# Twelve buffers for x tiles, weight casts ahead of tile 1, four tiles transposed on TensorE in a hybrid encoder block

## The chip, the cores and the metric

The kernel runs on one core of one Trainium2 chip. The metric is the device time of one execution, in microseconds (us). Most executions of a kernel agree within 0.3%.

## What is computed

One layer of a bidirectional encoder. The rows of x (2048 x 1024) are normalised and multiplied by one wide matrix; its columns give a Fourier branch, a branch of dilated window attention (24 heads in three configurations), and gates; an output projection and the residual follow.

```python
hn = rms_norm(h, norm_w)
proj = hn @ w_in.astype(jnp.float32)
u_f, g_f, q, k, v, g_a = jnp.split(proj, SPLIT_POINTS, axis=-1)
...
q = rms_norm(q.reshape(B, S, N_ATTN_HEADS, HEAD_DIM), q_norm_w) * HEAD_DIM ** -0.5
k = rms_norm(k.reshape(B, S, N_ATTN_HEADS, HEAD_DIM), k_norm_w)
...
for c, (window, dilation) in enumerate(DILATED_CONFIGS):
    o_c, lse_c = dilated_window_attention(q[:, :, sl], k[:, :, sl], v[:, :, sl], window, dilation, slopes)
...
y_a = o * jax.nn.silu(g_a)
mixed = jnp.concatenate([y_f, y_a], axis=-1) @ w_out.astype(jnp.float32)
h = h + mixed
```

## The kernel before

The 2048 rows of x are 16 tiles of 128 rows. Each float32 operand of a large product is split into two float16 halves, a high one and a low one, and the product is the sum of three: high by high, low by high, high by low. For that the normalised x must lie transposed in `xT`, both halves (j = 0 and 1) of all 16 tiles.

**A tile of x** goes through these steps. `x_load` (L174) brings it into the float32 buffer `xs` by a DMA from SP; `xs` has six places and tile r takes place r % 6. `x_sq` (L187) squares it on ScalarE and sums each row. `x_rs` makes the reciprocal root of the sums on VectorE, in 11 small steps (L195, L105 to L112), for a group of tiles that `xgrp` names: tile 0 alone, 1 and 2, 3 alone, then pairs. `x_hi` (L210) writes the high half on ScalarE, `x_lo` (L218) the low half on VectorE. A half is transposed either on TensorE, eight blocks of 128 x 128 (`x_tr`, L225) and an eviction to `xT` (`x_ev`, L230) on ScalarE or VectorE, or by a transposing DMA from SP (`x_dt`, L233). Tiles 0 and 1 take TensorE for both halves; from tile 2 on the high half takes TensorE and the low half the DMA.

**A unit** is two heads of one configuration: 384 columns of w_in. Its weights are eight tiles of 128 rows (k = 0 to 7): `w_load` (L243) brings them from SP, `w_prep` reduces them to one scale (L259 to L278: a reduce for each tile, a small matmul into `pm`, the scale `nws`) and writes the high halves on ScalarE (L284) and the low halves on VectorE (L286). `w_prep` is a generator of 20 steps. `inproj(u, t)` (L307) then makes 24 matmuls of 128 x 384 for tile t, of about 0.16 us each at full clock, into one of three `psq` buffers. For tile 0 of unit 0 they come in the order high by high (8), low by high (8), high by low (8); otherwise k by k.

**The order is written out by hand.** A start-up block works tile 0, the weights of unit 0 and tile 1 by single steps (`go(...)` takes one step of a generator). After it one loop runs over all products, iteration i holding `inproj` number i; unit 0 is iterations 0 to 15. Each iteration takes the steps of many stages in a fixed order: the value half and the sums of tile i - 1 (L318 to L346), the low half's DMA, the high and low halves of tile i + 3, two or three transposes between the matmuls, queries and keys of tile i - 6 (L359 to L371 on GpSimd and ScalarE, transposed by DMA at L380 and copied across partitions at L401), and from iteration 14 the attention of unit 0 (`att_s` at L444 and L456 on TensorE, `att_max` at L474, `att_exp` at L492, `att_hi`, `att_lo`, and the DMA at L509). The function `plan` says how many steps of the next unit's `w_prep` each iteration takes: for unit 1 it begins at iteration 2, with 14 iterations left. Each engine and each issuing queue takes its instructions in this order.

`gains` (L154 to L170) makes the key gains on VectorE, writes them to DRAM (`KD`) and reads them back to all partitions (`kb`) by DMAs from SP.

**Areas.** `xs` lies in the first of two areas with the tag `st`; the units' transposed queries and keys (`st`) take the two in turn.

```python
self.xs = self.stp.tile([128, 3, 2, S], F16, name="xs", tag="st", bufs=2)
```

The attention of a unit, the other branch and the output follow in the loop and in `tail_`; the change does not touch them.

Of the kernel before, what the change touches and what calls it, by code (L numbers as in the profile page):

```python
# [24 lines left out]
NT = 16  # L25
# [51 lines left out]
def plan(n):  # L77
    if n == 14:
        return [3, 3, 2, 1, 0, 1, 0, 1, 2, 2, 2, 1, 1, 1]
    if n < 12:  # L80
        return [4, 4, 1, 1, 1, 3, 3, 3]
    head = [2, 2, 2, 2, 1, 1, 1] if n == 16 else [3, 3, 2, 1, 1, 1]
    m = n - len(head)
    return head + [9 // m + (i < 9 % m) for i in range(m)]
# [6 lines left out]
class Kernel:  # L91
# [81 lines left out]
    def x_load(self, r):  # L173
        self.nc.sync.dma_start(self.xs[:, r % 6], self.a["x"][0, r * 128:r * 128 + 128])  # L174

    def xgrp(self, r):
        return ((0, 1), (1, 2), (1, 2), (3, 1))[r] if r < 4 else (r - r % 2, 2)

    def x_sq(self, r):
        r0, n = self.xgrp(r)  # L180
        if r == r0:
            self.XS[r0] = self.sm.tile([128, 2], F32, name="xss", bufs=6)
            self.XR[r0] = self.sm.tile([128, 2], F32, name="xri", bufs=6)
        junk = self.wk.tile([128, 2, 256], F32, name="xjk", tag="P", bufs=2)
        junk = junk.rearrange("p a d -> p (a d)").bitcast(F16)
        o = r - r0
        self.nc.scalar.activation(junk, self.xs[:, r % 6], AF.Square, accum_out=self.XS[r0][:, o:o + 1])  # L187
# [16 lines left out]
    def x_hi(self, r):  # L204
        nc = self.nc
        t = self.xs[:, r % 6]
        ri = self.x_ri(r)
        hl = [self.wk.tile([128, D], F16, name="xhl", tag="pp", bufs=4) for _ in range(2)]
        self.XH[r] = hl
        nc.scalar.activation(hl[0], t, AF.Copy, scale=ri)  # L210

    def x_lo(self, r):
        nc = self.nc
        t = self.xs[:, r % 6]
        ri = self.x_ri(r)
        hl = self.XH[r]
        E = nc.vector
        E.scalar_tensor_tensor(hl[1], t, ri, hl[0], op0=OP.mult, op1=OP.subtract)  # L218

# [8 lines left out]
    def x_ev(self, r, j):  # L228
        E = self.nc.scalar.copy if r == 0 or (r + j) % 2 == 0 else self.nc.vector.tensor_copy
# [698 lines left out]
    def body(self):  # L928
# [3 lines left out]
        with ExitStack() as ctx:  # L932
# [18 lines left out]
            self.xs = self.stp.tile([128, 3, 2, S], F16, name="xs", tag="st", bufs=2)  # L951
            self.xs = self.xs.rearrange("p a b s -> p (a b s)").bitcast(F32).rearrange("p (r d) -> p r d", d=D)
# [7 lines left out]
            for r in (4, 5):  # L960
                self.x_load(r)
# [11 lines left out]
            self.x_sq(1)  # L973
# [3 lines left out]
            self.x_load(6)  # L977
            self.x_sq(2)
# [4 lines left out]
            self.x_ev(0, 1)  # L983
            g1 = self.x_rs(1)
            for _ in range(9):
                go(wg, g1, g1)
            for _ in g1:
                pass
            self.x_hi(1)
            self.x_lo(1)  # L990
            self.x_load(7)
# [34 lines left out]
            xd, xl, xt = [], [], [1]  # L1026
            ng = og = iter(())
            self.YD = []
            for i in range(max(len(items) + 1, G + 32)):
                ip, wchunks = iter(()), 0  # L1030
                if i < len(items):
                    u, _, _, gen, out = items[i]
                    ip = gen()
# [3 lines left out]
                    if u == 0 and p < 2:  # L1037
                        for k in range(4 * p, 4 * p + 4):
                            self.w_load(1, k)
                    p0 = 2 if u == 0 else 0  # L1040
# [20 lines left out]
                for r in xd:  # L1061
                    self.x_dt(r)
# [4 lines left out]
                for r in xl:  # L1067
                    if r + 6 < NT and r > 1:
                        self.x_load(r + 6)
                xl = xd  # L1070
# [54 lines left out]
                for r in xt:  # L1125
                    for j in range(2 if r == 1 else 1):
# [3 lines left out]
                for r in xd:  # L1130
                    self.x_lo(r)
                chain(2)
                next(ip, None)
                if i == 0:
                    self.x_sq(4)
                    self.x_sq(5)
                if i + 6 < NT:
# [127 lines left out]
```

## Time and profile before

| | us |
|---|---|
| median of three runs | 1427.89 (1427.65 to 1429.28) |
| the profiled execution | 1427.95 |
| span of the profiled execution | 1426.2 |
| TensorE busy | 1390.3 |
| VectorE busy | 986.7 |
| ScalarE busy | 739.4 |
| GpSimd busy | 458.6 |

How it is read: PE is TensorE, DVE VectorE, ACT ScalarE, POOL GpSimd, SP the queue that issues most DMAs. A row of the timeline gives the start, the time taken, engine, line, operation, what is written from what, the number of instructions, and in brackets the idle time of the engine just before it and what ended that. A row of the waits gives who waited for whom: us in total, times, longest. A row of the windows gives, for a stretch, the busy us of PE, PE's weight loads, DVE, ACT and POOL with the number of instructions, then the granted TensorE clock, the share of the DMA engines and GB/s.

### The profile page before, as it was taken

The numbers are of one execution on the slowest core, as the hardware profiler recorded it, in microseconds if no ns is written. First come the engines' busy times: TensorE is split into PE (matmuls) and PEld (weight loads), VectorE is DVE, ScalarE is ACT, GpSimd is POOL, SyncE is SP. The second block draws the span as 40 slices with busy tenths as digits, with TensorE's granted clock in tenths as the row PEclk, the third lists the DMA queues.
The fourth block names the chain that finished last, engine by engine and source line by source line (L and its number), as shares of the span: only waits on it lengthen the run. The fifth ranks groups of instructions, "written<-read, shape, count | busy, mean of one in ns | idle before, by whom it ended". The sixth has DMA issues, their size and how long they took to land.

```text
span 1426.2 us, 27743 instructions
## 1 busy us (share of the span) xinstructions
PE 1390.3 (97%) x9554; PEld 1027.6 (72%) x9554; DVE 986.7 (69%) x3130; ACT 739.4 (52%) x2079; POOL 458.6 (32%) x637
## 2 busy tenths in 40 slices
PE   4999999999999999999999999999999998999998
PEld 2666666667777777778888888744448697788887
DVE  6798888887878888888877777744488776611111
ACT  6676767676766666666756666554213134300110
POOL 0254444444444444444443333320000002211110
PEclk9999999999999999999999999999999999999999
DMA  7777777676766768687846465654434237333332
GB/s 212 201 142 128 143 127 142 130 140 133 136 140 121 150 117 158 119 158 115 150 101 136 99 135 97 137 110 129 147 120 136 89 102 264 103 112 111 111 117 76
DMA packets 409485, 188.66 MB, mean 132 GB/s; under 512 B 304832, under 2 KB 391040, under 8 KB 408832
## 3 DMA queue, kind: packets, MB, share of 16 engines
q1 hardware_dynamic: 380740, 173.89, 54.5%
q10 hardware_dynamic: 28604, 13.00, 3.9%
q8 instruction: 75, 1.23, 0.4%
q14 instruction: 66, 0.54, 0.1%
HBM read 72.37 MB, written 29.76 MB: 72 GB/s over the span
## 4 chain that ended last, share of the span: by engine, by line
PE 83%; DVE 6%; DMA 5%; ACT 2%; issue 2%; POOL 1%; SPq 1%; ACTq 0%; POOLq 0%; DVEq 0%
PE psq L307 44%; PE py L917 12%; PE psq L569 12%; PE psq L585 6%; PE pS L456 3%; PE po L522 2%; DMA wor<-in_w_out_dram 2%; PE po L523 1%; DMA xs<-in_x_dram 1%; PE pS L444 1%; DVE xhl L218 1%; DMA pt<-ph 1%; DMA qw<-qw 1%; DVE wh L286 1%; ACT xjk L187 0%
## 5 line engine op out<-in xcount | busy, mean ns | idle before, releaser
L307 PE MATMUL psq<-wh,xT 128*128 128x384 f16 x4608 | 789.5, 327 | 8.2 <-ACT wh L284 4.2
L307 PEld LDWEIGHTS <-xT 128*128 128x128 f16 x4608 | 541.0, 119 | 200.1 <-issue 7.1
L492 ACT ACTIVATE P<-pS,ob,kb 128x256 f32<-128x256 f32 (+1 forms) x384 | 199.4, 526 | 150.2 <-DVE ob L484 149.8
L504 POOL TENSOR_TENSOR ph<-P,ph 128x512 f16<-128x512 f32 x160 | 189.1, 1182 | 193.8 <-ACT ph L499 171.5
L360 POOL TENSOR_TENSOR qn<-qn,kb 128x128 f32<-128x128 f32 x192 | 87.5, 456 | 295.5 <-DVE qn L359 195.9
L917 PE MATMUL py<-wo,mx 128*128 128x512 f32 x768 | 181.3, 395 | 0.4 <-DVE mx L896 0.4
L569 PE MATMUL psq<-xT,wh 128*128 128x512 f16 x768 | 168.9, 379 | 0.0
L474 DVE CUSTOM_DVE_ANT_0 pS<-pS,bt 128x256 f32<-128x256 f32 (+1 forms) x384 | 147.8, 385 | 28.2 <-PE pS L444 19.8
L917 PEld LDWEIGHTS py<-wo,mx 128*128 128x128 f32 x768 | 143.2, 188 | 32.3 <-DVE mx L896 0.8
L371 POOL TENSOR_TENSOR hl<-qn,hl 128x256 f16<-128x256 f32 x192 | 130.7, 681 | 30.2 <-ACT hl L366 30.2
L569 PEld LDWEIGHTS <-wh 128*128 128x128 f16 x768 | 74.2, 98 | 87.0 <-issue 0.8
L920 DVE TENSOR_TENSOR xo<-xo,py 128x512 f32<-128x512 f32 x32 | 22.0, 688 | 139.1 <-PE py L917 139.1
L533 DVE TENSOR_REDUCE ob<-po 128x128 f32<-128x256 f32 (+1 forms) x160 | 75.3, 470 | 55.4 <-PE po L523 55.4
L499 ACT CAST ph<-P 128x512 f16<-128x512 f32 x160 | 99.0, 619 | 8.7 <-DMA wr<-in_w_in_dram 1.3
L366 ACT CAST hl<-qn 128x256 f16<-128x256 f32 x192 | 77.1, 402 | 47.6 <-POOL qn L360 37.0
L327 DVE TENSOR_TENSOR vt<-psq,vt 128x128 f16<-128x128 f32 x192 | 55.0, 286 | 62.2 <-ACT vt L326 62.0
L326 ACT CAST vt<-psq 128x128 f16<-128x128 f32 x192 | 51.2, 267 | 82.5 <-PE po L523 82.5
L286 DVE SCALAR_TENSOR_TENSOR wh<-wr,nws,wh 128x384 f16<-128x384 f32 x128 | 86.6, 682 | 2.6 <-ACT wh L284 2.6
L895 ACT CAST mx<-pya 128x512 fp32r<-128x512 f32 x16 | 9.4, 587 | 148.0 <-issue 124.9
L585 PE MATMUL psq<-wh,xT 128*128 128x256 f16 x768 | 84.3, 273 | 0.0
L585 PEld LDWEIGHTS <-xT 128*128 128x128 f16 x768 | 75.2, 98 | 9.1
L318 ACT COPY raw<-psq 128x256 f32<-128x256 f32 x192 | 69.3, 361 | 21.1 <-PE psq L307 20.6
(158 smaller groups left out, 1774.9 us busy)
## 6 DMA issues: line engine op xcount, KB each, us to landing
wr<-in_w_in_dram SPq DMA_DIRECT2D x104, 192.0 KB, 2.8
ot<-O SPq DMA_DIRECT2D x16, 792.0 KB, 4.6
st<-st SPq DMA_DIRECT2D x96, 128.0 KB, 2.6
xs<-in_x_dram SPq DMA_DIRECT2D x16, 512.0 KB, 5.3
xo<-in_x_dram SPq DMA_DIRECT2D x16, 512.0 KB, 3.5
out_dram<-xo SPq DMA_DIRECT2D x15, 512.0 KB, 2.9
O<-ob ACTq DMA_DIRECT2D x108, 66.0 KB, 2.6
O<-ob ACTq DMA_DIRECT2D x32, 132.0 KB, 2.4
```

Of the source, the lines that this page charges most:

```text
L286: V.scalar_tensor_tensor(wh[:, 1, k - 1, :n], wr[k - 1], nws[:, k - 1:k], wh[:, 0, k - 1, :n], op0=OP.mult, op1=OP.subtract)
L307: nc.tensor.matmul(ps[:, :384], self.xtile(j, k, c, t), wh[:, l, k, :384], start=n == 0, stop=n == 23)
L360: G.tensor_tensor(qn[:, 2:4], qn[:, 2:4], self.kf[:, h0:h0 + 2], OP.mult)
L366: self.nc.scalar.copy(hl.rearrange("p a h l d -> p (a h) l d")[:, :, 0], qn)
L371: self.nc.gpsimd.tensor_tensor(hv[:, :, 1], qn, hv[:, :, 0], OP.subtract)
L474: V.tensor_tensor_reduce(out=sS[:, h, cs], in0=ps[:, h, cs], in1=bs, scale=1.0, scalar=-3.0e38, op0=OP.add, op1=OP.max, accum_out=mx[:, e, ...
L492: self.nc.scalar.activation(P[:, h, cs], sS[:, h, cs], AF.Exp, bias=ob[:, e, 130 + h:131 + h], scale=self.om[:, h0 + h:h0 + h + 1], accum_ ...
L499: self.nc.scalar.copy(ph[:, 0], P)
L504: self.nc.gpsimd.tensor_tensor(ph[:, 1], P, ph[:, 0], OP.subtract)
L569: nc.tensor.matmul(ps, wh[:, l, k, col * 128:col * 128 + 128], self.xT[:, j, k, ch * 512:ch * 512 + 512], start=n == 0, stop=n == 23)
L585: nc.tensor.matmul(ps[:, j * 256:j * 256 + 256], self.xT[:, i, k, r * 128:r * 128 + 128], wh[:, l, k, 128:384], start=n % 24 == 0, stop=n ...
L917: nc.tensor.matmul(ps[nh], m[:, j, k], wo[nh][k][:, l], start=(j, l, k) == (0, 0, 4), stop=(j, k) == (1, 3))
```

## The change

`xs` becomes a list of two areas of six places, so that twelve tiles of x have room; both areas of `st` hold x first. Tiles 0 to 11 are loaded ahead of the loop; tiles 12 to 15 follow when the low halves of tiles 6 to 9 are written. Tiles 0 to 3 each have a reciprocal root of their own, and both their halves are transposed on TensorE; the evictions alternate between ScalarE and VectorE from tile 0 on. In the start-up the casts of unit 0's weights come ahead of tile 1's steps, and half of tile 0's matmuls ahead of tile 1's transposes. The weight loads of unit 1 move from iterations 0 and 1 to iterations 3 to 6, and its preparation begins at iteration 6.

```diff
 def plan(n):
     if n == 14:
         return [3, 3, 2, 1, 0, 1, 0, 1, 2, 2, 2, 1, 1, 1]
+    if n == 10:
+        return [3, 3, 2, 1, 1, 1, 2, 2, 2, 3]
...
     def x_load(self, r):
-        self.nc.sync.dma_start(self.xs[:, r % 6], self.a["x"][0, r * 128:r * 128 + 128])
+        self.nc.sync.dma_start(self.xtl(r), self.a["x"][0, r * 128:r * 128 + 128])
+
+    def xtl(self, r):
+        return self.xs[r >= 6][:, r % 6]
 
     def xgrp(self, r):
-        return ((0, 1), (1, 2), (1, 2), (3, 1))[r] if r < 4 else (r - r % 2, 2)
+        return (r, 1) if r < 4 else (r - r % 2, 2)
...
     def x_ev(self, r, j):
-        E = self.nc.scalar.copy if r == 0 or (r + j) % 2 == 0 else self.nc.vector.tensor_copy
+        E = self.nc.scalar.copy if (r + j) % 2 == 0 else self.nc.vector.tensor_copy
         E(self.xT[:, j, :, r * 128:(r + 1) * 128], self.XP.pop((r, j)))
...
-            self.xs = self.stp.tile([128, 3, 2, S], F16, name="xs", tag="st", bufs=2)
-            self.xs = self.xs.rearrange("p a b s -> p (a b s)").bitcast(F32).rearrange("p (r d) -> p r d", d=D)
+            self.xs = []
+            for _ in range(2):
+                t = self.stp.tile([128, 3, 2, S], F16, name="xs", tag="st", bufs=2)
+                self.xs.append(t.rearrange("p a b s -> p (a b s)").bitcast(F32).rearrange("p (r d) -> p r d", d=D))
...
-            for r in (4, 5):
+            for r in range(4, 12):
                 self.x_load(r)
             wg = self.w_prep(0)
...
             self.x_hi(0)
             self.x_tr(0, 0)
-            self.x_sq(1)
             go(wg, wg, wg, wg, wg, wg)
             go(wg)
             self.x_lo(0)
-            self.x_load(6)
-            self.x_sq(2)
             self.x_ev(0, 0)
             go(wg)
             self.x_tr(0, 1)
             go(wg)
             self.x_ev(0, 1)
+            ip0 = self.inproj(0, 0)
+            go(wg, wg)
+            self.x_sq(1)
             g1 = self.x_rs(1)
-            for _ in range(9):
-                go(wg, g1, g1)
-            for _ in g1:
-                pass
+            for _ in range(3):
+                go(wg, g1, g1, g1, g1)
+            go(wg, wg)
+            go(wg)
+            go(ip0, ip0)
             self.x_hi(1)
             self.x_lo(1)
-            self.x_load(7)
+            self.x_tr(1, 0)
+            self.x_ev(1, 0)
+            self.x_sq(2)
+            go(wg)
+            self.x_tr(1, 1)
+            self.x_ev(1, 1)
+            go(ip0)
+            for _ in self.x_rs(2):
+                pass
             self.x_sq(3)
             xg = self.x_rs(3)
...
-                    ip = gen()
+                    ip = gen() if i else ip0
...
-                    if u == 0 and p < 2:
-                        for k in range(4 * p, 4 * p + 4):
+                    if u == 0 and 3 <= p < 7:
+                        for k in range(2 * p - 6, 2 * p - 4):
                             self.w_load(1, k)
-                    p0 = 2 if u == 0 else 0
+                    p0 = 6 if u == 0 else 0
...
                 for r in xd:
-                    self.x_dt(r)
+                    if r > 3:
+                        self.x_dt(r)
...
-                for r in xl:
-                    if r + 6 < NT and r > 1:
-                        self.x_load(r + 6)
-                xl = xd
...
                 for r in xt:
-                    for j in range(2 if r == 1 else 1):
+                    for j in range(2 if r < 4 else 1):
                         self.x_tr(r, j)
                         self.x_ev(r, j)
                 xt = xd
                 for r in xd:
                     self.x_lo(r)
+                    if 6 <= r < 10:
+                        self.x_load(r + 6)
...
-                if i == 0:
-                    self.x_sq(4)
-                    self.x_sq(5)
-                if i + 6 < NT:
+                if i < 2:
+                    self.x_sq(2 * i + 4)
+                    self.x_sq(2 * i + 5)
+                elif i + 6 < NT:
                     self.x_sq(i + 6)
```

The steps `x_sq`, `x_hi` and `x_lo` read their tile through `xtl` too. Lines of the changed file are five higher than before from `x_sq` on.

**ScalarE in the start-up.** Before, from the high half of tile 0 on; `xjk` is a sum of squares (of tiles 1 and 2, later of 3), `xhl` a high half, `xT` an eviction, `wh` a weight cast:

```order
L210 ACTIVATE xhl<-xs,xri 128x1024
L187 ACTIVATE xjk,xss<-xs 128x1024 x2
L230 COPY xT<-xps 128x8x128 x2
L284 ACTIVATE wh<-wr,nws 128x384 x8
L210 ACTIVATE xhl<-xs,xri 128x1024
L187 ACTIVATE xjk,xss<-xs 128x1024
L210 ACTIVATE xhl<-xs,xri 128x1024
L230 COPY xT<-xps 128x8x128
L187 ACTIVATE xjk,xss<-xs 128x1024 x3
```

Now, from the same high half to the eviction of tile 2:

```order
L215 ACTIVATE xhl<-xs,xri 128x1024
L235 COPY xT<-xps 128x8x128
L289 ACTIVATE wh<-wr,nws 128x384 x2
L192 ACTIVATE xjk,xss<-xs 128x1024
L289 ACTIVATE wh<-wr,nws 128x384 x6
L215 ACTIVATE xhl<-xs,xri 128x1024
...
L215 ACTIVATE xhl<-xs,xri 128x1024
L192 ACTIVATE xjk,xss<-xs 128x1024 x2
L323 COPY raw<-psq 128x256
L324 ACTIVATE sq<-psq 128x256
L331 CAST vt<-psq 128x128
L215 ACTIVATE xhl<-xs,xri 128x1024
L235 COPY xT<-xps 128x8x128
```

The sums of tiles 1 and 2 and tile 0's second eviction stood ahead of the casts; now only the sum of tile 1 stands among them, behind the second, and the second eviction is VectorE's. The sums of tiles 4 and 5 and three steps of tile 0's product stand between the high half of tile 2 and the eviction of its transpose.

**SP at the same place.** Before; `xs` is a load of x, `wr` of weights, `xT` the transposing DMA (of tiles 2, 3, then 4 and 5):

```order
L174 DMA xs<-in_x_dram 128x1024 x7
L243 DMA wr<-in_w_in_dram 128x3x128 x8
L233 DMA_TRANSPOSE xT<-xhl 128x8x128
L167 DMA KD<-kt 24x67
L169 DMA kb<-KD 128x1608
L170 DMA dist<-in_dist_dram 128x640
L233 DMA_TRANSPOSE xT<-xhl 128x8x128
L174 DMA xs<-in_x_dram 128x1024
L233 DMA_TRANSPOSE xT<-xhl 128x8x128 x2
```

Now (the first `xT` are tiles 4 and 5):

```order
L176 DMA xs<-in_x_dram 128x1024 x11
L169 DMA KD<-kt 24x67
L171 DMA kb<-KD 128x1608
L172 DMA dist<-in_dist_dram 128x640
L248 DMA wr<-in_w_in_dram 128x3x128 x2
L238 DMA_TRANSPOSE xT<-xhl 128x8x128 x2
L176 DMA xs<-in_x_dram 128x1024
L248 DMA wr<-in_w_in_dram 128x3x128 x2
L238 DMA_TRANSPOSE xT<-xhl 128x8x128
```

The transposes of tiles 2 and 3 are gone from SP, unit 1's loads stand in pairs from iteration 3 on, and each reload of x stands ahead of a pair and the next transpose.

**VectorE in iterations 14 and 15.** Before; `vt` and `ss` belong to the last product, `wh` is a low half of unit 1's weights, `pS` the scores:

```order
L327 TENSOR_TENSOR vt<-psq,vt 128x128
L337 TENSOR_REDUCE ss<-sq 128x4
L286 SCALAR_TENSOR_TENSOR wh<-wr,nws,wh 128x384
L474 ISA pS,mx<-pS,bt 128x256
...
L484 TENSOR_TENSOR ob<-mx,kb 128x2
L327 TENSOR_TENSOR vt<-psq,vt 128x128
L337 TENSOR_REDUCE ss<-sq 128x4
L286 SCALAR_TENSOR_TENSOR wh<-wr,nws,wh 128x384
```

Now:

```order
L332 TENSOR_TENSOR vt<-psq,vt 128x128
L342 TENSOR_REDUCE ss<-sq 128x4
L291 SCALAR_TENSOR_TENSOR wh<-wr,nws,wh 128x384 x2
L479 ISA pS,mx<-pS,bt 128x256
...
L489 TENSOR_TENSOR ob<-mx,kb 128x2
L332 TENSOR_TENSOR vt<-psq,vt 128x128
L342 TENSOR_REDUCE ss<-sq 128x4
L291 SCALAR_TENSOR_TENSOR wh<-wr,nws,wh 128x384 x3
```

Five low halves stand in these two iterations where two stood.

More of the change, by code (lines that the diff above doesn't have):

```diff
@@ L186, in x_sq @@
         o = r - r0
-        self.nc.scalar.activation(junk, self.xs[:, r % 6], AF.Square, accum_out=self.XS[r0][:, o:o + 1])
+        self.nc.scalar.activation(junk, self.xtl(r), AF.Square, accum_out=self.XS[r0][:, o:o + 1])
     def x_rs(self, r0):
@@ L205, in x_hi @@
         nc = self.nc
-        t = self.xs[:, r % 6]
+        t = self.xtl(r)
         ri = self.x_ri(r)
@@ L213, in x_lo @@
         nc = self.nc
-        t = self.xs[:, r % 6]
+        t = self.xtl(r)
         ri = self.x_ri(r)
@@ L1025, in body @@
             ao = ao2 = ao3 = None
-            xd, xl, xt = [], [], [1]
+            xd, xt = [], []
             ng = og = iter(())
```

## The prediction

> **What bounds the kernel now.** I read the page's busy shares, then TensorE's waits, then its timeline with the granted clock, and last what held the queues it waited for.
>
> ```profile
> PE 1390.3 (97%) x9554; PEld 1027.6 (72%) x9554; DVE 986.7 (69%) x3130; ACT 739.4 (52%) x2079; POOL 458.6 (32%) x637
> PE xps L225 <- ACT xhl L210: 10.4, 1, 10.4
> PE psq L307 <- ACT wh L284: 4.2, 1, 4.2
> PE psq L307 <- DMA xT<-xhl: 3.2, 1, 3.2
> ...
> 18.92 5.29 PE L307 MATMUL psq<-wh,xT 128*128 128x384 f16 x12 [4.24 <-ACT wh L284]
> 25.62 0.62 PE L225 MATMUL xps<-idh,xhl 128*128 128x128 f16 x8 [0.55 <-DVE xss L195]
> 26.08 4.06 PE L307 MATMUL psq<-wh,xT 128*128 128x384 f16 x24
> ...
> 33.11 0.34 PE L307 MATMUL psq<-wh,xT 128*128 128x384 f16 x1 [0.58 <-ACT xT L230]
> 36.63 3.70 PE L307 MATMUL psq<-wh,xT 128*128 128x384 f16 x11 [3.18 <-DMA xT<-xhl]
> ...
> 46.59 4.18 PE L307 MATMUL psq<-wh,xT 128*128 128x384 f16 x24
> ...
> 106.55 0.50 PE L456 MATMUL pS<-st 128*128 128x256 f16 x3 [0.58 <-DMA st<-st]
> ```
>
> TensorE is busy for 97%, and all its waits that this change can reach lie ahead of 107 us. So the change is worth what it does to the start. 24 matmuls take 3.9 us from start to start of what follows (0.163 each). The row at 46.59 is the second half of tile 3 with the first half of tile 4, and behind it no wait stands until 106.55; I measure the gain at this row.
>
> ```profile
> 34.00:36.00 2.00, 0.00 (x0) 0.00 (x0) 1.79 (x14) 1.34 (x6) 0.00 (x0) 0.95 0.96 93
> 36.00:38.00 2.00, 1.37 (x5) 0.68 (x6) 0.63 (x4) 1.76 (x2) 0.00 (x0) 0.50 0.11 40
> ...
> 42.00:44.00 2.00, 2.00 (x12) 1.14 (x11) 1.99 (x2) 0.00 (x0) 0.00 (x0) 0.84 0.94 303
> ```
>
> The column of the granted clock (third from the right) shows that the 3.18 us wait also cost speed: half clock from about 35.8 (0.95 over two us) to about 42.6 (0.84). From 36.63 to 42.6 that loses 3.0 us. With both waits of tile 2 this stall costs 3.2 + 0.6 + 3.0 = 6.8 us.
>
> ```profile
> 25.59 0.33 SPq L174 DMA_DIRECT2D xs<-in_x_dram  x1
> 25.97 4.39 SPq L243 DMA_DIRECT2D wr<-in_w_in_dram  x8
> 30.46 2.19 SPq L233 DMA_TRANSPOSE xT<-xhl  x1
> 34.61 0.39 SPq L167 DMA_DIRECT2D KD<-kt  x1
> 36.80 0.37 SPq L169 DMA_DIRECT2D kb<-KD  x1
> ...
> DMA to landing us min/median/max: 3.1/3.5/5.3
> 14.05 1.06 ACT L187 ACTIVATE xjk<-xs 128x1024 f16<-128x1024 f32 x1 [3.70 <-DMA xs<-in_x_dram]
> ...
> 16.45 1.91 ACT L230 COPY xT<-xps 128x1024 f16<-128x1024 f16 x2
> 18.25 4.16 ACT L284 ACTIVATE wh<-wr,nws 128x384 f16<-128x384 f32 x8
> ...
> 44.39 1.06 ACT L187 ACTIVATE xjk<-xs 128x1024 f16<-128x1024 f32 x1 [6.63 <-DMA xs<-in_x_dram]
> ```
>
> On SP the transpose of tile 2's low half stood behind x tile 7 and eight weight loads, and landed 6.1 us after its issue (30.46 to 36.6). ScalarE waited for x tiles 1 and 2 before the casts (18.25), and 6.63 us for x tile 8.
>
> **The change, part by part.** I walk the queues in the new order with these durations, each engine in order.
>
> ```profile
> 14.21 0.23 DVE L271 TENSOR_SCALAR nws<-nw,scb 128x8 f32<-128x8 f32 x1
> 15.40 1.15 ACT xjk L187 x2
> 22.69 1.67 DVE L286 SCALAR_TENSOR_TENSOR wh<-wr,nws,wh 128x384 f16<-128x384 f32 x3
> 22.81 1.15 ACT L210 ACTIVATE xhl<-xs,xri 128x1024 f16<-128x1024 f32 x1 [0.41 <-DVE xri L112]
> 24.28 1.28 DVE L218 SCALAR_TENSOR_TENSOR xhl<-xs,xri,xhl 128x1024 f16<-128x1024 f32 x1
> 26.31 0.68 DVE L230 COPY xT<-xps 128x1024 f16<-128x1024 f16 x1
> 31.14 0.29 DVE L327 TENSOR_TENSOR vt<-psq,vt 128x128 f16<-128x128 f32 x1 [1.91 <-ACT vt L326]
> 32.89 1.27 DVE L218 SCALAR_TENSOR_TENSOR xhl<-xs,xri,xhl 128x1024 f16<-128x1024 f32 x1
> ```
>
> That is 1.15 for a sum of squares or a high half on ScalarE, 0.96 for its eviction (1.91 / 2), 0.52 for a cast (4.16 / 8); on VectorE 1.25 for a low half, 0.65 for an eviction, 0.55 for a weight's low half, 0.195 for a small step of a reciprocal root, and 1.75 for the group from 31.14 to 32.89.
>
> *Weights first.* Nothing changes up to the scale nws (14.44). ScalarE then casts two weight tiles (14.5), squares tile 1 (15.55), and casts six (16.7 to 19.9). TensorE's first matmul comes at 15.1 instead of 18.92, but it only follows the casts. The reciprocal root of tile 1 ends on VectorE at 20.0, its high half on ScalarE at 21.25, its low half at 22.9 and its second transpose at 24.0. So the 24 matmuls of 26.08 begin at 24.0: 2.1 us won, not 3.8.
>
> *Tiles 2 and 3 on TensorE, root by root.* Two more transposes of eight (0.45 each from start to start, 25.62 to 26.08: 0.9 us on TensorE), one eviction more for each, and one more root of 11 small steps (2.1 us of VectorE). Root 2 ends at 26.2, high half 2 at 27.4, low half 2 at 28.7, root 3 at 29.9. ScalarE has two sums of squares (to 29.65), tile 0's three steps (0.8), high half 3 (31.6), eviction of tile 2 (32.5). VectorE evicts the other half behind its 1.75 us group at 32.95. Tile 2 starts at **33.0** instead of 36.63, after a wait of some 1.7 us. Should the clock still be half while TensorE works on tiles 0 and 1 (0.32 a matmul up to about 30), this wait hides it.
>
> Tile 3: low half at 34.15, transposes done at 35.9, tile 2 ends at 37.8. ScalarE meanwhile has sums 6 and 7, tile 1's steps, high halves 4 and 5 (37.8), then the eviction (38.75). Tile 3 starts at **38.8** after a wait of 1.0. Its first half (1.95) and two transposes (0.9) end at 41.65, where the row of 46.59 then stands: **4.9 us won**. Waits of 1.7 and 1.0 are shorter than the 3.18 that halved the clock, so I charge nothing for it.
>
> The Trainium skill, "TensorE: Matmul & The Clock Gate", Part 1, says that the clock falls after about one idle window of some 3.4 us and that the window runs freely. The 6.8 us at half clock are two such windows, so the trace agrees; by that rule too the two shorter waits cost no clock.
>
> *Loads of x.* Twelve go out ahead of everything else but unit 0's weights.
>
> ```profile
> 8.34 6.97 DMA xs<-in_x_dram
> 20.00:22.00 2.00, 1.89 (x5) 0.40 (x5) 1.91 (x8) 2.00 (x5) 0.00 (x0) 1.00 0.00 0
> ```
>
> Tile 2 landed at 15.3, 1.3 us after tile 1 (14.0); from 20 to 22 the DMA moved nothing. At that pace tile 11 lands at 27, and ScalarE first squares tile 8 at 38.75 in the walk. So the waits like the one at 44.39 go; were a tile late, ScalarE's 6.63 bounds the price. This term sits inside the 4.9.
>
> *Weight loads of unit 1, SP.* KD still goes at 34.6 and its copy kb at 36.8, behind them the broadcast and two weight loads, then the transpose of tile 4, whose low half ends at 38.9. It needs to land by 43.6. Bounds: 3.1 us (no wait) to the 6.1 seen for tile 2 (wait 1.5, to 45.1). I take 5.3, the longest in the view, since kb's 804 KB move beside it: landing at 44.2, **0.5 us lost**.
>
> *Reduces and casts of unit 1 later.* No instruction is added. Eight reduces (0.55 each) move from iterations 2 to 4 into 6 to 8; the casts' low halves move from 10 to 15 into 12 to 15.
>
> ```profile
> 51.87 0.29 DVE L327 TENSOR_TENSOR vt<-psq,vt 128x128 f16<-128x128 f32 x1 [1.48 <-ACT vt L326]
> 76.42 1.45 DVE L218 SCALAR_TENSOR_TENSOR xhl<-xs,xri,xhl 128x1024 f16<-128x1024 f32 x1
> 81.70 4.06 PE L307 MATMUL psq<-wh,xT 128*128 128x384 f16 x24
> 90.00:100.00 10.00, 10.00 (x71) 6.39 (x70) 9.76 (x29) 6.43 (x20) 4.96 (x7) 1.00 0.97 182
> ```
>
> Tile 3's value half at 51.87 was 3.3 us behind the start of tile 4 (46.59 + 1.95), because ScalarE had waited for x. In the walk ScalarE evicts tile 4 until 43.4, squares tile 9 (44.55) and takes tile 3's three steps (45.35), so it comes at 45.5, 1.9 behind 43.6: 1.4 us of lag less. Tile 12's low half ends at 77.9 and tile 12 starts at 83.65 (12 matmuls into 81.70); with 3.5 for the DMA 2.3 us are spare. So 3.7 us cover the 4.4 us of reduces that now stand nearer to it. Bounds: nothing (VectorE idles somewhere between, as it did for 1.48 ahead of 51.87) to 0.7. I take **nothing**, nearer to that row; without the cover each us of lag is a us on TensorE. The 0.58 us wait at 106.55 is at the end of the same chain (VectorE, ScalarE, GpSimd, two DMAs); with 1.4 us less lag it goes: **0.6 won** (0 to 0.6).
>
> *Areas and table.* The second area holds x until iteration 12; unit 1's transposed queries and keys need it from iteration 23. The reload of x tile 12 on SP waits for tile 6's low half, and behind it stand two weight loads and tile 6's transpose, which waits for the same low half. Nothing is charged.
>
> **Sum.** 4.9 - 0.5 + 0.6 = 5.0 us off the span of 1426.2. The profiled execution took 1427.95, the median of the runs is 1427.89, so both give 1422.9.
>
> **Rivals.**
> *No stall at all at the start.* If the walk is too slow on ScalarE, TensorE streams from 24.0: 72 matmuls (11.7) and six transposes (2.7) reach the row of 46.59 at 38.4, 8.2 won, with the 0.6 **1419.1**. Against it: ScalarE is full from 15 to 38 in the walk.
> *ScalarE becomes the bound.* Its queue now holds four sums of squares ahead of the evictions of tiles 2 and 3. If each of the two waits is a us longer, 3.0 are won: **1425.0**, on the edge.
> *The stall only moves.* If tile 4's transposed half lands over 3 us late, behind kb and weights, the 6.8 us stall stands at tile 4: 5.5 - 6.8, **1429.2**, no difference to be told. It needs 8 us to land; tile 2's took 6.1 behind more traffic.
> *Transposes do not run at full clock.* Each group of eight then costs about 1.05 and not 0.45; four groups after 33 cost 2.4 more: **1425.3**. The row at 25.62 (0.62 for eight) speaks against it.
> The Trainium skill, same page, Part 4, states just this, that the full clock does not engage for transposes; this trace disagrees at 25.62.
> *Slower: VectorE bounds the end of unit 0.* It is 9.76 of 10 us busy from 90 to 100. If it gains nothing in absolute time, the low halves of iterations 14 and 15 (five where two stood, three times 0.6) put the copy st<-st 1.8 us later than 106.5, and TensorE, there early and waiting over 3 us, pays 3.4 us of half clock: **1433.1**. It decides where VectorE's lag stays at the 3.3 us of 51.87 plus the full 4.4 of reduces. Against it: the row below, idle time which the walk fills.
>
> ```profile
> 41.22 0.69 DVE L230 COPY xT<-xps 128x1024 f16<-128x1024 f16 x1 [4.52 <-PE xps L225]
> ```
>
> **How the numbers follow.** 0.2% is 2.9 us, about what a measurement can tell from no change. Forecast 0.58 (1421.4 to 1424.5), no stall 0.07, ScalarE 0.12 (half of it on each side of the edge), stall moved 0.11, transposes 0.03, of which I count all as no difference, slower 0.09. Faster: 0.58 + 0.07 + 0.06 = 0.71; same: 0.06 + 0.11 + 0.03 = 0.20; slower 0.09. The range leaves out the slower case, half of the moved stall and half of the best case: 1420.2 to 1428.2.
>
> **What would show it.** In the new profile: first input matmul near 15.1; the wait for the DMA xT<-xhl at tile 2 gone, waits of some 1.7 and 1.0 us for evictions in its place; granted clock 1.00 from 30 on; the row of 46.59 near 42; no sum of squares waiting for x; tile 4 started near 44; no wait at 106.55. A half clock after 40, or VectorE's low halves of tiles 11 to 15 later against their tiles, would make it wrong.

## The result, and the profile after

| | before | after |
|---|---|---|
| median of five runs | 1427.89 us (1427.65 to 1429.28) | 1420.33 us (1419.29 to 1421.96) |
| profiled execution, its span | 1427.95, 1426.2 | 1421.88, 1420.1 |

The ratio is 0.9944 (95% interval 0.9933 to 0.9956): faster by 8.0 us of 1427.9, 6.3 to 9.6, which gives 1419.9. The forecast was 5.0 us: 1422.9, in a range of 1420.2 to 1428.2. The same changed kernel, run twice more, gave 0.9942 (0.9929 to 0.9955) and 0.9953 (0.9939 to 0.9966). The two first profiles differ by 6.1 us.

TensorE's waits after (us in total, times, longest) that answer to those shown of before:

```profile
PE psq L312 <- ACT wh L289: 1.5, 2, 1.1
PE psq L312 <- ACT xT L235: 1.5, 2, 0.8
PE xps L230 <- DVE xhl L223: 1.0, 2, 0.6
```

The wait of 4.2 for the casts is 1.5, and the one of 3.2 for the DMA is gone; short waits for evictions and one low half are new. TensorE's timeline shows where they stand:

```profile
15.29 0.98 PE L312 MATMUL psq<-wh,xT 128*128 128x384 f16 x2 [0.45 <-ACT wh L289]
...
23.14 4.06 PE L312 MATMUL psq<-wh,xT 128*128 128x384 f16 x24
27.04 0.61 PE L230 MATMUL xps<-idh,xhl 128*128 128x128 f16 x8
28.29 0.62 PE L230 MATMUL xps<-idh,xhl 128*128 128x128 f16 x8 [0.64 <-DVE xhl L223]
...
31.69 0.34 PE L312 MATMUL psq<-wh,xT 128*128 128x384 f16 x1 [0.83 <-ACT xT L235]
32.19 1.96 PE L312 MATMUL psq<-wh,xT 128*128 128x384 f16 x11 [0.16 <-DVE xT L235]
...
37.78 1.96 PE L312 MATMUL psq<-wh,xT 128*128 128x384 f16 x11 [0.62 <-ACT xT L235]
39.58 1.06 PE L230 MATMUL xps<-idh,xhl 128*128 128x128 f16 x16
40.47 4.06 PE L312 MATMUL psq<-wh,xT 128*128 128x384 f16 x24
...
119.51 0.49 PE L461 MATMUL pS<-st 128*128 128x256 f16 x3 [0.64 <-DMA st<-st]
```

The row that stood at 46.59 stands at **40.47**: 6.12 us won where 4.9 were forecast. Eight transposes take 0.61 us and sixteen 1.06. No wait for `st` stands any more where the one of 106.55 stood, just behind the first `po` row; one of 0.64 us stands at 119.51, where there was none before. The windows after, with the granted clock in the third column from the right:

```profile
34.00:36.00 2.00, 2.00 (x24) 1.57 (x23) 1.79 (x12) 1.78 (x4) 0.00 (x0) 1.00 0.02 3
36.00:38.00 2.00, 1.38 (x10) 0.65 (x8) 2.00 (x3) 2.00 (x3) 0.00 (x0) 1.00 0.99 306
42.00:44.00 2.00, 2.00 (x14) 1.16 (x13) 0.74 (x1) 2.00 (x7) 0.00 (x0) 1.00 0.53 105
```

SP's queue after at this place, and below it the landing times of its transposes:

```profile
35.11 0.35 SPq L171 DMA_DIRECT2D kb<-KD  x1
...
37.69 3.52 SPq L238 DMA_TRANSPOSE xT<-xhl  x2
...
DMA to landing us min/median/max: 3.3/4.2/4.6
```

The clock is full where it was half. Tile 4's transposing DMA goes out at 37.69, 1.2 us earlier than in the walk, and lands within 4.6 us, by 42.3; tile 4 starts at 42.42 (40.47 + 1.95). It is just in time.

### The profile page after: what moved, and what is told of

It reads as the page before. It is cut to its first block, busy times and chain, and to the rows that moved or that the text cites. A ratio compares the mean times of both kernels' runs of the same rounds, so it can differ in the third digit from the quotient of the medians.

```text
span 1420.1 us, 27783 instructions
## 1 busy us (share of the span) xinstructions
PE 1389.2 (98%) x9570; PEld 1027.6 (72%) x9570; DVE 988.3 (70%) x3143; ACT 739.9 (52%) x2079; POOL 459.8 (32%) x637
## 4 chain that ended last, share of the span: by engine, by line
PE 84%; DVE 5%; DMA 4%; issue 2%; POOL 2%; ACT 1%; SPq 1%; POOLq 0%; DVEq 0%; ACTq 0%
PE psq L312 45%; PE py L922 12%; PE psq L574 12%; PE psq L590 6%; PE pS L461 4%; PE po L527 2%; DMA wor<-in_w_out_dram 2%; PE po L528 1%; PE pS L449 1%; DVE xhl L223 1%; POOL ph L509 1%; PE pya L899 0%; DVE wo L873 0%; POOL hl L376 0%; PE ptr L774 0%
## 5 line engine op out<-in xcount | busy, mean ns | idle before, releaser
L376 POOL TENSOR_TENSOR hl<-qn,hl 128x256 f16<-128x256 f32 x192 | 134.1, 698 | 30.7 <-ACT hl L371 30.7
```

The lines of the kernel that those rows point to most:

```text
L376: self.nc.gpsimd.tensor_tensor(hv[:, :, 1], qn, hv[:, :, 0], OP.subtract)
```

## The experiments

Ratios are to the kernel before on the same chip, with 95% intervals; "row" is the start of the 24 matmuls that make the second half of tile 3 and the first of tile 4 (46.59 before, 40.47 after). Four kernels take one part back from the changed kernel, four put one part alone into the kernel before.

### One part taken back

**f5_castslate**, the old start-up:

```diff
+            self.x_sq(1)
             go(wg, wg, wg, wg, wg, wg)
...
-            for _ in range(3):
-                go(wg, g1, g1, g1, g1)
...
-            self.x_tr(1, 0)
-            self.x_ev(1, 0)
...
-            xd, xt = [], []
+            xd, xt = [], [1]
```

> The changed kernel with the start-up in the old order: the sums of tiles 1 and 2 ahead of the casts of unit 0's weights, tile 1's transposes between tile 0's matmuls in iteration 0; places, early loads, transposes on TensorE and the later weights of unit 1 stay. Theory: tile 0 starts near 17.5 to 19 instead of 15.3, tile 1's and with it tile 2's high half come later, and 1 to 3 us of the 6.1 won at the start go: 1421.5 to 1423.5. Rival, ScalarE is full from 15 to 38 and does the same work in either order, so that tile 3 starts when it did: within 0.5 us of the changed kernel.

Measured 0.9963 (0.995 to 0.9975). TensorE's timeline:

```profile
18.13 5.30 PE L312 MATMUL psq<-wh,xT 128*128 128x384 f16 x12 [2.77 <-ACT wh L289]
...
42.40 4.38 PE L312 MATMUL psq<-wh,xT 128*128 128x384 f16 x24
```

The row comes 1.93 us later, by the ratio 2.7: the theory holds. Of the 2.84 us by which tile 0 starts later two thirds reach tile 4.

**e1_dma23**, the low halves of tiles 2 and 3 by DMA again:

```diff
-                    if r > 3:
+                    if r > 1:
                         self.x_dt(r)
...
-                    for j in range(2 if r < 4 else 1):
+                    for j in range(2 if r < 2 else 1):
```

> The changed kernel, with the low halves of tiles 2 and 3 transposed by DMA again (their root of their own, the early loads and the free SP stay). Theory, SP's queue was the stall: what held tile 2's transpose before was x tile 7 and eight weight loads ahead of it on SP. Those are gone, so it is issued near 28.2 and lands within 3.5 us, near 31.7, as tile 2 wants it; tile 3's stands behind KD's write and lands near 38 to 40, a wait of up to 2 us. Clock full throughout the start; 1420 to 1422.5. Rival, the stall comes with the transposing DMA itself: it lands 6 us after its issue whoever stands ahead, TensorE waits over 3 us at tile 2 or 3, the clock halves, and the time is 1425 to 1427.

Measured 0.9982 (0.9973 to 0.9991), 1426.94 us. SP's queue and the landing times of its transposes:

```profile
28.03 2.06 SPq L238 DMA_TRANSPOSE xT<-xhl  x1
...
34.28 0.36 SPq L171 DMA_DIRECT2D kb<-KD  x1
...
35.16 1.24 SPq L238 DMA_TRANSPOSE xT<-xhl  x1
...
DMA to landing us min/median/max: 3.0/3.3/6.0
```

TensorE at tile 3:

```profile
36.23 0.34 PE L312 MATMUL psq<-wh,xT 128*128 128x384 f16 x1 [0.25 <-DVE xT L235]
41.12 3.33 PE L312 MATMUL psq<-wh,xT 128*128 128x384 f16 x11 [4.55 <-DMA xT<-xhl]
```

The place is the theory's, the price the rival's: tile 2's half is in time, tile 3's goes out 2.7 us after it is written (32.5), behind KD and kb, and lands 6.0 us later.

**e7_kdlater** has, besides, the key gains one iteration later:

```diff
-                        if 0 < i < NT:
+                        if 1 < i < NT:
                             next(kg, None)
```

> The run e1_dma23 with the key gains one iteration later, so that KD's write, kb's 804 KB and the distances stand behind tile 3's transposing DMA on SP and not ahead of it. In e1_dma23 that DMA was issued at 35.16, right behind kb, and tile 3 waited 4.55 us for it; tile 2's, alone on SP at 28.03, made TensorE wait for nothing. Theory, what stands ahead on SP and in the DMA engines makes it late: it is issued near 34, lands within 3.5 us, tile 3 waits under 1.5 us, the clock stays full, 1420 to 1422.5. Rival, a transposing DMA in this stretch needs 6 us whatever stands ahead of it: tile 3 still waits over 3 us, 1425 to 1427.

Measured 1.0002 (0.9994 to 1.0011). SP's queue:

```profile
28.27 5.29 SPq L238 DMA_TRANSPOSE xT<-xhl  x2
...
41.05 0.36 SPq L171 DMA_DIRECT2D kb<-KD  x1
...
43.55 3.91 SPq L238 DMA_TRANSPOSE xT<-xhl  x2
```

TensorE at tiles 3 and 4:

```profile
36.94 2.12 PE L312 MATMUL psq<-wh,xT 128*128 128x384 f16 x12 [0.70 <-DVE xT L235]
...
48.64 3.37 PE L312 MATMUL psq<-wh,xT 128*128 128x384 f16 x11 [5.54 <-DMA xT<-xhl]
```

Tile 3 waits for no DMA: what stands ahead on SP made it late. But the time forecast is wrong: tile 4 is now the tile behind kb. Its low half is written near 38.1, its DMA goes out at 43.55, and TensorE waits 5.54 us. The stall follows kb.

**e2_six** and **e2b_six**, six places for x; the reload of tile r + 6 right behind low half r (first), or an iteration behind the transposing DMA, as before the change (second):

```diff
-        return self.xs[r >= 6][:, r % 6]
+        return self.xs[0][:, r % 6]
...
-            for r in range(4, 12):
+            for r in range(4, 6):
                 self.x_load(r)
...
-                    if 6 <= r < 10:
+                    if 2 <= r < 10:
                         self.x_load(r + 6)
```

> The changed kernel with six places for x instead of twelve: loads 6 and 7 go out behind the low halves of tiles 0 and 1, load r + 6 behind the low half of tile r. Theory, the second area matters little once SP has no weights in its queue: tile 8 is loaded from about 28.7, lands by 33, and its sum of squares is wanted at 37.6, so nothing waits in the start; 0 to 1 us slower than the changed kernel, 1420 to 1421.5. Rival, the early loads are what lets ScalarE run: its sums wait again as at 44.39 before (6.63 us), the evictions of tiles 3 and 4 stand behind them, and 2 to 4 us are lost, 1422.5 to 1424.5.

> The changed kernel with six places for x, as e2_six, but with the reloads in the place that they had before the change: the load of tile r + 6 an iteration behind the transposing DMA of tile r, not ahead of it. In e2_six tile 4 waited 4.89 us for its transposed half behind two reloads (1 MB). Theory, the order on SP decides and not the number of places: tile 4's transpose goes ahead of the reloads, TensorE waits under 1 us for it, and at most the sums of tiles 10 and 11 wait on ScalarE: 1420 to 1422.5. Rival, six places are too few in either order (a reload is late for its sum, its evictions late for TensorE): 1424 to 1428.

Measured 0.9986 (0.9977 to 0.9995) and 0.9989 (0.998 to 0.9998). TensorE at tile 4 in e2_six:

```profile
47.81 3.51 PE L312 MATMUL psq<-wh,xT 128*128 128x384 f16 x11 [4.89 <-DMA xT<-xhl]
```

ScalarE at the sum of tile 8 in e2b_six:

```profile
42.56 1.06 ACT L192 ACTIVATE xjk<-xs 128x1024 f16<-128x1024 f32 x1 [4.45 <-DMA xs<-in_x_dram]
```

TensorE at tile 4 in e2b_six:

```profile
46.41 3.63 PE L312 MATMUL psq<-wh,xT 128*128 128x384 f16 x12 [3.44 <-ACT xT L235]
```

Both theories are wrong, and so is e2_six's rival, by its time and by its wait; e2b_six's rival holds. With six places either the reloads delay tile 4's transposed half, or tile 8's load is late and the eviction of tile 4 stands behind its sum. Twelve places take x out of that stretch.

**e3_wearly**, unit 1's weights early again:

```diff
-                    if u == 0 and 3 <= p < 7:
-                        for k in range(2 * p - 6, 2 * p - 4):
+                    if u == 0 and p < 2:
+                        for k in range(4 * p, 4 * p + 4):
                             self.w_load(1, k)
-                    p0 = 6 if u == 0 else 0
+                    p0 = 2 if u == 0 else 0
```

> The changed kernel with unit 1's eight weight loads back in iterations 0 and 1 and its preparation from iteration 2. Theory: the loads stand on SP ahead of tile 4's transpose (eight, 4.4 us of issue), but behind KD; tile 4's half lands at up to 43.5 against the 40.3 at which tile 4 now starts, a wait of 0 to 3 us; and the reduces in iterations 2 to 4 keep VectorE's lag, so that a wait of about 0.6 us stands again where attention starts, near 100: 1421 to 1424. Rival, the later preparation won nothing and the SP queue has room: 1420.0 to 1420.6, the same rows as in the changed kernel.

Measured 0.9943 (0.993 to 0.9955): by the ratio the rival. The loads go out from 18.29 on, when SP has nothing else to do. This part wins nothing here. The rows are not quite the same, though: tile 4 waits 0.54 us for an eviction (43.10), and where attention starts no wait for `st` is left at all.

### One part alone, on the kernel before

f3_casts is the change without the edits of e1, e2b and e3. The cores of the other three, f2_transposes, f4_places and f1_wlate:

```diff
-                    for j in range(2 if r == 1 else 1):
+                    for j in range(2 if r < 4 else 1):
...
-            for r in (4, 5):
+            for r in range(4, 12):
                 self.x_load(r)
...
-                    if u == 0 and p < 2:
+                    if u == 0 and 3 <= p < 7:
```

> The kernel before with the new start-up alone: the casts of unit 0's weights ahead of tile 1's sum, half of tile 0's matmuls ahead of tile 1's transposes, a root for each of tiles 0 to 3; six places, the reloads, unit 1's early weights and the transposing DMAs of tiles 2 and 3 as before. Theory: tile 0 starts near 15.3 and tile 1 some 2.9 us earlier, and the stall at tile 2 or 3 takes it all back, since SP's queue sets when the transposed halves land: 0.998 to 1.001. Rival, the parts add up: f5_castslate lost 0.0019 without it, so it wins 0.0015 to 0.002 here: 0.998 or below with the wait at tile 2 no longer than 3.2 us.

> The kernel before with one part of the change alone: the low halves of tiles 2 and 3 are transposed on TensorE. Theory, one stall of about 7 us is handed on until every tile's transposed half is in time: the wait at tile 2 goes, but the sum of tile 8 still waits for its load and tile 4's transposing DMA stands behind kb and loads of x, so a wait of over 3 us stands at tile 4, with half clock behind it: ratio 0.997 to 1.001. Rival, the parts add up: this part takes away the 6.8 us of tile 2's stall, less 0.9 for the transposes and some for the later start: 0.9955 to 0.9965.

> The kernel before with twelve places for x and tiles 0 to 11 loaded ahead of the loop, alone. The loads of x no longer stand between the casts and SP's queue, so the eight weight loads go out from about 18 as in e3_wearly, and tile 2's transposing DMA has SP to itself near 30. Theory: tile 2 starts near 34 without a DMA wait over 2 us, but tile 3's transpose stands behind KD and kb as in e1_dma23 and the stall of 4 to 5 us with half clock stands there: 0.997 to 1.000. Rival, the early loads alone take the stall away: 0.995 to 0.9965.

> The kernel before with unit 1's weight loads in iterations 3 to 6 and its preparation from iteration 6, alone. Theory: SP is free when tile 2's low half is written (near 30.3), its transposing DMA lands 3.5 to 4.5 us later and TensorE waits 1 to 2 us less at tile 2; but tile 3's stands behind KD and kb, as in e1_dma23, and the wait of 4 to 5 us with half clock stands there: ratio 0.998 to 1.001. Rival: with no weights in the DMA engines either half is in time and 2 us or more are won, 0.9985 or less, up to the 0.9955 of the whole stall.

| alone | ratio (95%) | the stall |
|---|---|---|
| start-up, f3 | 0.9981 (0.9973 to 0.999) | tile 2, for the DMA |
| transposes, f2 | 0.9991 (0.9981 to 1.0) | tile 4, for an eviction |
| places, f4 | 0.9997 (0.9988 to 1.0006) | tile 3, for the DMA |
| weights later, f1 | 0.9999 (0.999 to 1.0008) | tile 3, for the DMA |

TensorE's rows with the stall in f3:

```profile
31.51 0.34 PE L312 MATMUL psq<-wh,xT 128*128 128x384 f16 x1 [2.15 <-ACT xT L235]
33.73 3.70 PE L312 MATMUL psq<-wh,xT 128*128 128x384 f16 x11 [1.88 <-DMA xT<-xhl]
```

The same in f2:

```profile
48.16 2.96 PE L307 MATMUL psq<-wh,xT 128*128 128x384 f16 x12 [3.27 <-ACT xT L230]
```

In f4:

```profile
42.31 3.64 PE L310 MATMUL psq<-wh,xT 128*128 128x384 f16 x11 [4.04 <-DMA xT<-xhl]
```

And in f1:

```profile
42.68 3.70 PE L309 MATMUL psq<-wh,xT 128*128 128x384 f16 x11 [4.67 <-DMA xT<-xhl]
```

Alone the parts win 0.0032 together, the change 0.0056; only f3's interval lies wholly below 1. f2, f4 and f1 bear the theory out: each hands the stall on to a later tile. In f2 the eviction at tile 4 is late because it stands on ScalarE behind the sum of tile 8, which waited 4.28 us for its load. f3 lies between its two forecasts: it wins 0.0019 (2.7 us), as f5 lost, though tile 2 still waits, 2.15 us for an eviction and 1.88 for the DMA.

### Where the rest comes from

The profiles show 6.1 us, the ratios about 8. Two more runs of the changed kernel and three more profiles of the kernel before, nothing edited:

> The changed kernel once more, beside the runs of this call. What its profile lost and won adds up to 6.1 us at tile 3 and 0.6 where attention starts, 6.7 of 1428, a ratio of 0.9953; the first runs gave 0.9944 (0.9933 to 0.9956). Theory, the trace's 6.7 us are all of it and the rest is spread of the runs (small waits for DMAs between 300 and 700 us differ by some 2 us from one profile to the next): 0.9948 to 0.9955. Rival, more is won than the start and attention show: 0.9940 to 0.9945 again.

> The kernel before, unchanged, for a second profile of it. Theory, its stall at the start varies: the row of 46.59 (second half of tile 3) comes at 46.6 to 50, on the mean over three profiles 1 to 2 us later than in the first one, and the first po row of attention later than 105.35 by as much. Rival, the start is the same to 0.4 us and the first profile is short elsewhere: from the first po row to the last 24 ptr matmuls it had 1095.8 us, where the kernels with other starts show 1094.9 to 1097.4.

> The kernel before, unchanged, third profile; as b0_before. The theory wants the mean of the three rows at 47.6 to 48.6, the rival at 46.2 to 47.0 with a middle stretch of 1096.5 or more.

> The kernel before, unchanged, fourth profile; as b1_before: the theory wants a row later than 47, the rival a middle stretch of 1096.5 us or more.

> The changed kernel, unchanged, beside the next run. Theory, the change shortens the stretch from the first po row to the last 24 ptr matmuls: 1094.9 to 1095.8 us again, ratio 0.9940 to 0.9946. Rival, that stretch spreads between 1095 and 1098 whatever the start: 1096.4 or more here or in the next run, and the mean of all profiles of the changed kernel's stretch is within 1 us of the mean for the kernel before (1097.4).

a0_again: its rival, 0.9942. a1_again gave 0.9953, which misses its forecast of 0.9940 to 0.9946. From the first `po` row of attention to the last 24 `ptr` matmuls (us), and the row:

| | row | first po | last ptr | stretch |
|---|---|---|---|---|
| before, first profile | 46.59 | 105.35 | 1201.15 | 1095.80 |
| b0, b1, b2 | 46.66, 46.65, 47.14 | 105.89, 106.31, 106.24 | 1203.87, 1204.21, 1204.13 | 1097.98, 1097.90, 1097.89 |
| after, first profile | 40.47 | 99.56 | 1194.54 | 1094.98 |
| a0, a1 | 40.78, 40.69 | 99.67, 99.59 | 1195.07, 1194.99 | 1095.40, 1095.40 |

In b0 and b1 tile 4 follows tile 3 after a wait of its own, 0.41 and 0.76. On the mean the row of b0 to b2 is 0.2 us later than in the first profile, the first po row 0.8, the stretch 2.1 longer: mostly the rival of b0. The first profile of the kernel before was a short one in attention, and there the change wins: 1097.4 us on the mean of four against 1095.3 of three, or 1095.8 with e4, e6 and e6_again, which are the same kernel there (1096.98, 1096.38, 1095.87). By the stretch that bears out a1's theory, with 1.6 us and a wide spread; three of the four profiles of the kernel before come from one chip, so it is not a firm number. To the first po row the means differ by 6.3 us (105.95 and 99.61), so start and stretch together give 7.9 us, about what the ratios show. What differs in the stretch is waiting for DMAs; a row of TensorE's timeline in b0:

```profile
713.60 0.23 PE L522 MATMUL po<-vt,pt 128*128 128x128 f16 x1 [0.89 <-DMA pt<-ph]
```

The totals of such waits in b0:

```profile
PE pS L456 <- DMA qw<-qw: 3.0, 4, 1.6
PE po L522 <- DMA pt<-ph: 1.9, 3, 0.9
```

And in a1:

```profile
PE pS L461 <- DMA qw<-qw: 1.8, 5, 0.7
PE po L527 <- DMA pt<-ph: 0.9, 2, 0.5
```

The wait at 713.60 sorts all profiles. It stands between 708 and 715 us, 0.56 to 0.89 long, in each of the nine whose low halves of tiles 2 and 3 are transposed by DMA (before four times, f1, f3, f4, e1, e7), and in none of the eleven that transpose them on TensorE. e1 has no other edit against the changed kernel and gets the wait; f2 has no other edit against the kernel before and loses it. So two DMAs fewer at 30 us change which of attention's DMAs come late near 711 us. On the mean the stretch is 1097.0 us in the nine and 1095.9 in the eleven, but f2's is 1097.3, as long as before, so this wait is not all of it. How the one does the other stays open.

### The tail

TensorE waits some 7 us for VectorE in the tail, before and after, and works at half clock behind it. 52 or 30 added matmuls keep it busy:

```diff
+            if s == 3 and nt == 3:
+                jk = self.psm.tile([128, 512], F32, name="pm", tag="m")
+                for n in range(52):
+                    nc.tensor.matmul(jk[:, n % 4 * 128:n % 4 * 128 + 128], self.F[s][:, n % 4, 0:128],
+                                     self.BD[:, s % 2, n % 4], start=True, stop=True)
```

> The changed kernel with 52 added matmuls (128 x 128, float32) whose result nobody reads, ahead of the last eight ptr matmuls near 1197.4, where TensorE waits 7.12 us for VectorE; at the 0.118 us that such a matmul takes at full clock they last 6.1 us. Theory, the clock: the wait halves the clock for 6.8 or 10.2 us behind it, so 3.4 to 5.1 us are lost there, and how many windows it takes splits the runs in two groups (1421.9 and 1419.3 to 1420.3). With TensorE busy through the wait the clock stays at 1.00, the time is 1415 to 1417.5 and the runs lie closer together. Rival, the time behind the wait is bound by VectorE and not by TensorE's clock: within 0.2% of the changed kernel, 1419 to 1422, and the two groups stay.

> The changed kernel with 30 added matmuls (128 x 128, float32, shown as 60, result read by nobody) ahead of the last eight ptr matmuls, where TensorE waits 7.12 us for VectorE. With 52 the clock stayed at 1.00 through the tail, but they took 11.78 us, 4.7 longer than the wait. Theory: 30 take 6.8 us, fit into the wait, the clock stays at 1.00, and 3.4 to 5.1 us of half-clock loss go: 1415 to 1417.5. Rival, what follows is bound by VectorE: 1419 to 1422.

> The kernel of e6_tailfit again (30 added matmuls ahead of the last eight ptr matmuls, result read by nobody), beside a1_again. Theory, a full clock in the tail is worth about half of the half-clock loss, since VectorE then bounds what follows (a wait of 1.19 us for mx stood there): 1.0 to 2.2 us below a1_again by medians, clock 1.00. Rival, it is worth nothing that can be told: within 0.7 us of a1_again.

Measured with 52: 0.996 (0.9948 to 0.9973); a matmul shows as two, so they took 11.78 us, 4.7 too long. With 30: 0.9939 (0.9923 to 0.9955) and 0.9941 (0.9928 to 0.9953), 1421.04 us beside 1421.93 in a1_again. A window after:

```profile
1206.00:1210.00 4.00, 4.00 (x12) 3.23 (x12) 2.07 (x4) 0.59 (x1) 3.19 (x3) 0.50 0.00 0
```

The same window with 30 (e6_tailfit):

```profile
1206.00:1210.00 4.00, 3.81 (x17) 3.08 (x17) 2.52 (x5) 0.85 (x2) 3.70 (x3) 1.00 0.00 2
```

And TensorE's timeline there:

```profile
1231.01 5.38 PE L927 MATMUL py<-wo,mx 128*128 128x512 f32 x22 [1.19 <-DVE mx L906]
```

The clock stays full, but TensorE then waits for VectorE (1.19 at mx, where the changed kernel waits 0.34). Both forecasts of 1415 to 1417.5 are wrong, and e6_tailfit's rival holds. e6_again lies 0.89 us below a1_again, between its two forecasts. So about 0.9 us may be left of the gain: these are the lowest ratios of all runs, and they cannot be told from those of the changed kernel. The five runs lie no closer together (1419.63 to 1422.75 in e6_tailfit, 1419.29 to 1421.96 in the changed kernel), so nothing shows that the clock in the tail makes their spread; that part of the theory fell.

## Why the prediction was too small

**The mechanism held.** What was forecast of the start is there: first input matmul at 15.29 (15.1), no DMA wait at tile 2, short waits for evictions in its place (0.99 and 0.62, forecast 1.7 and 1.0), full clock, no sum waiting for x. f5, e1 and e2 show that start-up, transposes and places are each needed. What failed is sizes of terms, and one term put at nothing. One argument was unsafe, though nothing came of it: that waits shorter than 3.18 us cost no clock. In f3 two waits of 2.15 and 1.88 with one matmul between them halved it.

**First step that failed: the 4.9 us of the walk.** It was 6.12. The walk's durations were too long, above all on ScalarE: sums and high halves were put at 1.15 us; from start to start they take 1.04 and 1.05. ScalarE's timeline after:

```profile
23.34 1.01 ACT L235 COPY xT<-xps 128x1024 f16<-128x1024 f16 x1 [1.40 <-PE xps L230]
...
25.76 1.15 ACT L215 ACTIVATE xhl<-xs,xri 128x1024 f16<-128x1024 f32 x1 [0.36 <-DVE xri L114]
26.82 1.04 ACT L192 ACTIVATE xjk<-xs 128x1024 f16<-128x1024 f32 x1
...
27.86 1.04 ACT L192 ACTIVATE xjk<-xs 128x1024 f16<-128x1024 f32 x1
...
30.62 1.01 ACT L235 COPY xT<-xps 128x1024 f16<-128x1024 f16 x1
```

Two waits stand in ScalarE's way up to 25.76, for TensorE and for VectorE, so it is not full from 15 to 38 as in the walk. Half of the error lies there: root 2 comes near 25.7 where the walk had 26.2, since tile 1's low half and transposes end earlier too (the 24 matmuls begin at 23.14, not 24.0). The other half is ScalarE's own: from high half 2 to the eviction of tile 2 it takes 4.86 us (25.76 to 30.62) where the walk had 5.4. The eviction ends at 31.6, 0.9 us ahead of the walk's 32.5, and all behind it comes 1.0 to 1.2 us earlier.

**Second: 0.5 us lost at tile 4** (44.2 less 43.6, so 0.6 by the walk's own figures). Nothing is lost: the low half was written 1.2 us earlier than in the walk, and 4.6 us to the landing were enough where 5.3 were taken. But e7 and e2_six show that the risk was real: the rival "the stall only moves" happens as soon as tile 4's DMA goes out later.

**Third: the later reduces and casts of unit 1, put at nothing, cost 0.6 us.** The 0.6 us at 106.55 were won as forecast. That wait was for the copies `st<-st`, and they now go out 3.83 us ahead of the first po row (99.56); before it was 2.43 (105.35): 1.4 us less lag, as in the walk. SP's queue before:

```profile
102.92 1.27 SPq L401 DMA_DIRECT2D st<-st  x2
```

And after:

```profile
95.73 1.29 SPq L406 DMA_DIRECT2D st<-st  x2
...
115.16 1.27 SPq L406 DMA_DIRECT2D st<-st  x2
```

The wait at 119.51 is another one, for the next pair of copies. In e3_wearly, where unit 1 is prepared early, this pair goes out 2.7 us sooner and no wait stands there:

```profile
112.48 1.26 SPq L406 DMA_DIRECT2D st<-st  x2
```

In this stretch VectorE is busy for 11.47 of 12 us after the change:

```profile
100.00:112.00 12.00, 12.00 (x93) 7.86 (x90) 11.47 (x42) 8.42 (x27) 6.58 (x11) 1.00 1.01 158
```

and for 9.84 in e3_wearly:

```profile
100.00:112.00 12.00, 12.00 (x97) 7.97 (x94) 9.84 (x36) 7.22 (x24) 7.12 (x12) 1.00 0.76 136
```

Such a wait, 19.6 to 20.1 us behind the first po row, stands in nine of the twelve profiles with the later preparation (not in e1, e7 and f1) and in none of the eight with the early one. e3_wearly pays 0.54 us at tile 4 instead, which fits its equal time. What was won at 106.55 is lost again at 119.51: in the first profiles the sum is 6.1, the start alone.

**Fourth, not in the sum:** some 1.6 us of attention's DMA waits. The prediction had said that behind the start only the wait at 106.55 could be reached.

The rivals: ScalarE did not become the bound. "VectorE bounds the end of unit 0" came true in small, with the 0.64 us of 119.51 and no half clock; from 90 to 100 VectorE worked 9.76 us before, and 8.07 from 84 to 94, where the same products stand now. "No stall at all" (1419.1) was nearest by time, by luck: 2.25 us of eviction and low-half waits remain at tiles 2 and 3, and part of the gain lies in attention.

The Trainium skill, "TensorE: Matmul & The Clock Gate", Part 4, says that the full clock does not engage for transposes; here, too, eight take 0.61 us at granted clock 1.00 and not the 1.05 of the rival that went by it: the trace disagrees again, and the measurement decides. Whether transposes alone would bring the clock up, no run here shows.

## What to carry to other kernels

A stall at the start of a pipeline is handed from tile to tile: find every queue that the next tile needs, and expect single fixes to win little and all of them together much (0.0032 against 0.0056 here). Ask of a large transfer such as kb who stands behind it after each change: moving it back an iteration (e7) freed tile 3 and stalled tile 4. One profile of a kernel is one draw: three more of the kernel before moved its middle stretch by 2.1 us, as much as a term of the sum.

## What the runs showed of the hardware

- Waits of TensorE of 3.2 to 5.5 us between 30 and 50 us (in f3 2.15 and 1.88 with one matmul between) were each followed by half clock, for 3.41 us (e1, e2, e2b, f2, f4, b1) or 6.83 us (before, b0, b2, e7, f1, f3); the 6.4 to 7.3 us in the tail by 6.83 or 10.24 us. The Trainium skill, "TensorE: Matmul & The Clock Gate", Part 1, gives a window of about 3.4 us that runs freely; these are one, two and three of them, and which number comes varies between runs of one kernel (10.24 and 6.83 in the tail of the changed kernel). The waits of 3.18 us (before) and of f3 are shorter than such a window, so the trace bears out its length, but not the prediction's reading that TensorE must be idle for a whole one.
- In e1 a transposing DMA lands 3.3 us after its issue by the median, and 6.0 right behind kb.
- With two more transposing DMAs near 30 us a wait of 0.56 to 0.89 us for another DMA stands near 711 us (nine profiles), without them it does not (eleven).
